# Moving middle blocks as two partition halves in 64 KB runs, from one buffer of three 2-row blocks

## The chip, the cores and the metric

The kernel runs on one core of a Trainium2 chip; the other cores are idle. The metric is the device time of one execution in microseconds (us). The four executions of the kernel before that stand against the changed kernel agree within 0.05%; over all rounds, which ran on several chips, it took 1247.99 to 1252.11 us (0.33%). The granted clock was 1.000. TensorE does next to nothing in this kernel (PE busy for 0.3 us), so that clock plays no part.

## The reference, cut to what matters

```python
def reference(logits, labels):            # (8, 1024, 8192) float32, (8, 1024) int32
    logits_max = np.max(logits, axis=-1, keepdims=True)
    exp_logits = np.exp(logits - logits_max)
    softmax = exp_logits / np.sum(exp_logits, axis=-1, keepdims=True)
    ...                                   # one_hot: 1.0 at labels
    return (softmax - one_hot).astype(np.float32)
```

There are 8192 rows of 8192 floats: 268.4 MB are read and 268.4 MB are written. Each row needs its maximum, its sum of exponentials, a scaling, and a subtraction at one place.

## The kernel before

A tile is 128 rows, one to each partition of SBUF (the memory on the chip that holds the tiles), 32 KB a row, 4 MB a tile. Six tiles fit the buffer. Loads are issued by the sync engine (SP), stores by ScalarE's queue (ACT). VectorE (DVE) does the maximum and the subtraction, ScalarE the exponential and the scaling.

```python
io = ctx.enter_context(tc.tile_pool(name="io", bufs=SLOTS))        # SLOTS = 6
def load(t):
    x = io.tile([P, V], fp32, tag="x", name="x")
    nc.sync.dma_start(out=x[:], in_=x_nv[t * P : (t + 1) * P, :])
    return x
def store(t, x):
    nc.scalar.dma_start(out=o_nv[t * P : (t + 1) * P, :], in_=x[:])
...                                       # row_max, exponent, inverse, normalize, subtract: cut
for t in range(T):                        # T = 64
    s = exponent(xs[t], ms[t])
    r = inverse(s)
    if t + 1 < T:
        xs[t + 1] = load(t + 1)           # waits until the tile six before it has been stored
        ms[t + 1] = row_max(xs[t + 1])
    if t > 0:
        store(t - 1, xs[t - 1])
    normalize(xs[t], r)
    subtract(t, xs[t])
```

## Time and profile before

| | before |
|---|---|
| time, median | 1248.12 us |
| DMA engines, share of the span (two queues) | 50.0% + 49.9% |
| DMA rate, mean | 431 GB/s |
| VectorE busy | 90% |
| one tile in the steady state | 19.35 us |

These are lines of the profile page: busy time, the slices (40 equal parts of the span, busy share in tenths), and the DMA queues (q1 holds the loads, q10 the stores; the last column is the time that their packets took, as a share of 16 engines' span).

```profile
PE 0.3 (0%) x1; PEld 0.2 (0%) x1; DVE 1122.1 (90%) x259; ACT 930.7 (75%) x257; POOL 4.1 (0%) x7
DMA  9999999999999999999999999999999999999998
GB/s 406 421 438 435 424 437 436 435 426 437 435 433 428 437 434 432 429 437 434 432 429 438 435 431 428 438 437 428 431 438 434 429 432 436 435 428 433 437 434 379
DMA packets 18519, 537.00 MB, mean 431 GB/s; under 512 B 2064, under 2 KB 2128, under 8 KB 2128
q1 hardware_dynamic: 9216, 268.44, 50.0%
q10 hardware_dynamic: 9296, 268.51, 49.9%
```

The reader is to see two things: the DMA engines have no idle time, and the rate hardly varies. Next come the waits: who waited for whom, us in total, times, longest. The first line is a compute engine's, the second the sync queue's.

```profile
DVE m L70 <- DMA x<-in_logits_dram: 83.7, 46, 2.4
...
SPq L65 <- DMA out_dram<-x: 1148.9, 58, 66.7
```

VectorE waits for loads only 83.7 us in all. Nearly all of the span, the sync queue waits for a store to land, because a store frees the buffer that the next load needs. A window of the steady state shows busy time by engine, then the granted clock, the DMA share and the rate:

```profile
core 0: us, PE busy (x) PEld busy (x) DVE busy (x) ACT busy (x) POOL busy (x), PEclk, DMA share, GB/s
310.00:620.00 310.00, 0.00 (x0) 0.00 (x0) 281.58 (x65) 235.52 (x66) 0.00 (x0) 1.00 1.00 433
```

In the single transfer records of this trace, a row of 32 KB took 1213 ns on its engine, a run of 1 KB took 46 ns, and a semaphore write 9 ns. A packet is one such run on one of the 16 DMA engines. From 310 to 1150 us 16 packets are in flight at 95% of the instants, and at half of the instants 13 or more of them go the same way, all loads or all stores.

### The profile page before, as it was taken

The page shows a single profiled execution, that of the slowest core. Times are in us where ns is not written, and L with a number is a line of the kernel's source. Part 1 is how long each engine was busy: PE and PEld are TensorE (multiplying, and loading weights), DVE is VectorE, ACT ScalarE, POOL GpSimd, SP SyncE. Part 2 cuts the span into 40 slices and gives each one's busy share as a digit, 9 for nine tenths or more (in the row PEclk, how much of TensorE's full clock was granted, in tenths as well). Part 3 has the DMA queues.
Part 4 walks back from the last instruction along what each step waited for, and adds up shares of the span by engine and source line. Part 5 has one row for each costly group of instructions (what it writes and reads, how often), then busy time and mean ns, then how long its engine had stood idle before and what let it go on. Part 6 is the DMA issues. An engine that isn't in the chain of part 4 may idle for free.

```text
span 1246.1 us, 997 instructions
## 1 busy us (share of the span) xinstructions
PE 0.3 (0%) x1; PEld 0.2 (0%) x1; DVE 1122.1 (90%) x259; ACT 930.7 (75%) x257; POOL 4.1 (0%) x7
## 2 busy tenths in 40 slices
PE   0000000000000000000000000000000000000000
PEld 0000000000000000000000000000000000000000
DVE  3999999999988989889898898988989989889893
ACT  3888888888877777777767777777777777777772
POOL 1000000000000000000000000000000000000000
DMA  9999999999999999999999999999999999999998
GB/s 406 421 438 435 424 437 436 435 426 437 435 433 428 437 434 432 429 437 434 432 429 438 435 431 428 438 437 428 431 438 434 429 432 436 435 428 433 437 434 379
DMA packets 18519, 537.00 MB, mean 431 GB/s; under 512 B 2064, under 2 KB 2128, under 8 KB 2128
## 3 DMA queue, kind: packets, MB, share of 16 engines
q1 hardware_dynamic: 9216, 268.44, 50.0%
q10 hardware_dynamic: 9296, 268.51, 49.9%
q14 instruction: 7, 0.06, 0.0%
HBM read 268.50 MB, written 268.44 MB: 431 GB/s over the span
## 4 chain that ended last, share of the span: by engine, by line
another core or an unknown queue 66%; DVE 21%; DMA 7%; issue 3%; SPq 1%; ACT 1%; DVEq 0%; ACTq 0%
DVE m L70 11%; DVE x L91 10%; DMA out_dram<-x 4%; DMA x<-in_logits_dram 3%; SPq L65 1%; ACT x L75 1%; DVEq L139 0%; ACT x L86 0%; DVE r L80 0%; ACTq L97 0%; DVEq L91 0%; DVEq L70 0%
## 5 line engine op out<-in xcount | busy, mean ns | idle before, releaser
L70 DVE TENSOR_REDUCE m<-x 128x1 f32<-128x8192 f32 x64 | 555.7, 8683 | 83.8 <-DMA x<-in_logits_dram 83.7
L75 ACT ACTIVATE x<-x,m 128x8192 f32<-128x8192 f32 x64 | 455.8, 7122 | 157.0 <-DVE m L70 157.0
L91 DVE SCALAR_TENSOR_TENSOR x<-iota,lab,x 128x4096 f32<-128x4096 int16 x128 | 567.9, 4479 | 4.1 <-ACT x L86 4.1
L86 ACT ACTIVATE x<-x,r 128x4096 f32<-128x4096 f32 x128 | 467.7, 3700 | 123.5 <-DVE r L80 123.5
L80 DVE RECIPROCAL r<-s 128x1 f32<-128x1 f32 x64 | 10.2, 159 | 7.3 <-ACT x L75 7.3
L75 ACT ACTIVATION_READ_ACCUMULATOR x<-x,m 128x1 f32 x64 | 12.0, 187 | 0.0
L75 ACT ACT_TABLE_LOAD x1 | 1.3, 1283 | 13.4 <-DMA x<-in_logits_dram 13.4
L56 DVE CAST lab_f<-lab_raw 64x128 f32<-64x128 int32 x1 | 0.2, 219 | 12.2 <-DMA lab_raw<-in_labels_dram 12.2
L46 POOL IOTA iota<- 128x4096 int16 x1 | 3.5, 3542 | 0.4 <-POOLq L128 0.4
L61 DVE TENSOR_SCALAR lab<-lab_ps 128x64 f32<-128x64 f32 x2 | 0.4, 220 | 0.5 <-PE lab_ps L58 0.5
L58 PE MATMUL lab_ps<-ident,lab_f 64*128 64x64 f32 x1 | 0.3, 338 | 12.5 <-DVE lab_f L56 12.5
L49 POOL TENSOR_SCALAR_AFFINE_SELECT ident<-ident 64x64 f32<-64x64 f32 x1 | 0.2, 234 | 0.1
L58 PEld LDWEIGHTS lab_ps<-ident,lab_f 64*128 64x128 f32 x1 | 0.2, 180 | 12.5 <-issue 12.5
L48 POOL MEMSET ident<- 64x64 f32 x1 | 0.1, 146 | 0.0
L128 POOL MEMSET const-bfloat16-1.0<- 128x1 bf16 x1 | 0.1, 107 | 0.0
L128 POOL MEMSET const-uint8-127<- 128x1 uint8 x1 | 0.1, 107 | 0.0
L128 POOL MEMSET const-float32-0.0<- 128x1 f32 x1 | 0.1, 104 | 0.2 <-issue 0.2
L128 POOL MEMSET const-float32-1.0<- 128x1 f32 x1 | 0.1, 104 | 0.0
## 6 DMA issues: line engine op xcount, KB each, us to landing
x<-in_logits_dram SPq DMA_DIRECT2D x64, 4096.0 KB, 24.2
out_dram<-x ACTq DMA_DIRECT2D x64, 4096.0 KB, 55.0
lab_raw<-in_labels_dram ACTq DMA_DIRECT2D x1, 64.0 KB, 11.4
```

The costliest lines, as they stand in the source:

```text
L46: nc.gpsimd.iota(iota[:], [[1, HALF]], base=0, channel_multiplier=0)
L49: nc.gpsimd.affine_select(out=ident[:], in_=ident[:], compare_op=Alu.not_equal, fill=1.0, base=0, pattern=[[-1, T]], channel_multiplier=1,)
L56: nc.vector.tensor_copy(out=lab_f[:], in_=lab32.rearrange("t (p s) -> t p s", s=step)[:, :, 0])
L58: nc.tensor.transpose(out=lab_ps[:], in_=lab_f[:], identity=ident[:])
L61: nc.vector.tensor_scalar_add(out=lab[:, c, :], in0=lab_ps[:], scalar1=float(-c * HALF))
L65: nc.sync.dma_start(out=x[:], in_=x_nv[t * P : (t + 1) * P, :])
L70: nc.vector.tensor_reduce(out=m[:], in_=x[:], axis=mybir.AxisListType.X, op=Alu.max, negate=True)
L75: nc.scalar.activation(out=x[:], in_=x[:], func=Act.Exp, bias=m[:], scale=1.0, accum_out=s[:])
L80: nc.vector.reciprocal(out=r[:], in_=s[:])
L86: nc.scalar.activation(out=xc, in_=xc, func=Act.Copy, bias=0.0, scale=r[:])
L91: nc.vector.scalar_tensor_tensor(out=xc, in0=iota[:], scalar=lab[:, c, t : t + 1], in1=xc, op0=Alu.is_equal, op1=Alu.subtract, reverse1=True,)
L128: nc = _bacc.Bacc("TRN2", target_bir_lowering=False, num_devices=1)
```

## The change

Partition p of a block now holds two neighbouring rows of the input, so one partition's share of a block is one contiguous run of 64 KB. Middle blocks move as two transfers of 64 partitions (0 to 63, 64 to 127). A half can be loaded again as soon as that half has been stored. Blocks 0 to 4 and 27 to 31 are loaded row by row, blocks 0, 1 and 24 to 31 stored so. Each of the buffer's three places for a block is called a slot. The intent is fewer and longer packets, with freeing fine enough to keep both directions going.

```diff
-SLOTS = 6
+SLOTS = 3
+G = 2
+Q = P // 2
...
+    x_b = x_nv.rearrange("(b p j) v -> b p j v", p=P, j=G)
...
+    X = io.tile([P, SLOTS, G, V], fp32)
+    rows = [(slice(0, P), slice(j, j + 1)) for j in range(G)]
+    halves = [(slice(0, Q), slice(0, G)), (slice(Q, P), slice(0, G))]
+    def parts(b, head, tail):
+        return rows if b < head or b >= B - tail else halves
+    def load(b):
+        for ps, js in parts(b, 5, 5):
+            nc.sync.dma_start(out=X[ps, b % SLOTS, js, :], in_=x_b[b, ps, js, :])
...
+    def store(t):
+        b, j = divmod(t, G)
+        pieces = parts(b, 2, 8)
+        if pieces is rows:
+            pieces = rows[j : j + 1]
+        elif j < G - 1:
+            return
+        for ps, js in pieces:
+            nc.scalar.dma_start(out=o_b[b, ps, js, :], in_=X[ps, b % SLOTS, js, :])
```

The compute instructions keep their shapes and their number; they work on one row of a block at a time. The labels are laid out for the new row order, which costs one small copy and one small matmul more.

More of the change, by code (lines that the diff above doesn't have):

```diff
@@ L31 @@
     T = N // P
+    B = T // G
     C = V // HALF
-    lab_tp = labels.rearrange("a b -> (a b)").rearrange("(t p) -> t p", p=P)
+    lab_bp = labels.rearrange("a b -> (a b)").rearrange("(b q) -> b q", q=G * P)
+    x_b = x_nv.rearrange("(b p j) v -> b p j v", p=P, j=G)
+    o_b = o_nv.rearrange("(b p j) v -> b p j v", p=P, j=G)
     const = ctx.enter_context(tc.tile_pool(name="const", bufs=1))
-    io = ctx.enter_context(tc.tile_pool(name="io", bufs=SLOTS))
+    io = ctx.enter_context(tc.tile_pool(name="io", bufs=1))
     stats = ctx.enter_context(tc.tile_pool(name="stats", bufs=4))
@@ L39 @@
     ctx.enter_context(tc.manual_schedule())
-    lab_raw = const.tile([T, P], labels.dtype)
-    nc.scalar.dma_start(out=lab_raw[:], in_=lab_tp)
+    lab_raw = const.tile([B, G * P], labels.dtype)
+    nc.scalar.dma_start(out=lab_raw[:], in_=lab_bp)
     iota = const.tile([P, HALF], i16)
     nc.gpsimd.iota(iota[:], [[1, HALF]], base=0, channel_multiplier=0)
-    ident = const.tile([T, T], fp32)
+    ident = const.tile([B, B], fp32)
     nc.gpsimd.memset(ident[:], 0.0)
@@ L50 @@
         out=ident[:], in_=ident[:], compare_op=Alu.not_equal, fill=1.0,
-        base=0, pattern=[[-1, T]], channel_multiplier=1,
+        base=0, pattern=[[-1, B]], channel_multiplier=1,
     )
-    lab_f = const.tile([T, P], fp32)
-    lab32 = lab_raw[:].bitcast(i32)
+    lab_f = const.tile([B, G, P], fp32)
     step = mybir.dt.size(labels.dtype) // 4
-    nc.vector.tensor_copy(out=lab_f[:], in_=lab32.rearrange("t (p s) -> t p s", s=step)[:, :, 0])
-    lab_ps = psum.tile([P, T], fp32)
-    nc.tensor.transpose(out=lab_ps[:], in_=lab_f[:], identity=ident[:])
@@ L59 @@
-    lab = const.tile([P, C, T], fp32)
-    for c in range(C):
-        nc.vector.tensor_scalar_add(out=lab[:, c, :], in0=lab_ps[:], scalar1=float(-c * HALF))
-    def load(t):
-        x = io.tile([P, V], fp32, tag="x", name="x")
-        nc.sync.dma_start(out=x[:], in_=x_nv[t * P : (t + 1) * P, :])
-        return x
-    def row_max(x):
+    lab32 = lab_raw[:].bitcast(i32).rearrange("b (p j s) -> b j p s", j=G, s=step)
+    lab = const.tile([P, C, G, B], fp32)
+    lab_ps = psum.tile([P, G, B], fp32)
@@ new lines @@
+    for j in range(G):
+        nc.vector.tensor_copy(out=lab_f[:, j, :], in_=lab32[:, j, :, 0])
+        nc.tensor.transpose(out=lab_ps[:, j, :], in_=lab_f[:, j, :], identity=ident[:])
+    for c in range(C):
+        nc.vector.tensor_scalar_add(out=lab[:, c], in0=lab_ps[:], scalar1=float(-c * HALF))
+    X = io.tile([P, SLOTS, G, V], fp32)
[3 more added lines that the diff above has]
+        return rows if b < head or b >= B - tail else halves
@@ L69, in row_max, with row, exponent @@
+    def load(b):
+        for ps, js in parts(b, 5, 5):
+            nc.sync.dma_start(out=X[ps, b % SLOTS, js, :], in_=x_b[b, ps, js, :])
+    def row(t):
+        return X[:, t // G % SLOTS, t % G, :]
+    def row_max(t):
         m = stats.tile([P, 1], fp32, tag="m", name="m")
-        nc.vector.tensor_reduce(out=m[:], in_=x[:], axis=mybir.AxisListType.X, op=Alu.max, negate=True)
+        nc.vector.tensor_reduce(out=m[:], in_=row(t), axis=mybir.AxisListType.X, op=Alu.max, negate=True)
         return m
-    def exponent(x, m):
+    def exponent(t, m):
@@ L74, in exponent @@
         s = stats.tile([P, 1], fp32, tag="s", name="s")
-        nc.scalar.activation(out=x[:], in_=x[:], func=Act.Exp, bias=m[:], scale=1.0, accum_out=s[:])
+        nc.scalar.activation(out=row(t), in_=row(t), func=Act.Exp, bias=m[:], scale=1.0, accum_out=s[:])
         return s
@@ L81, in inverse, with normalize, subtract @@
         return r
-    def normalize(x, r):
+    def normalize(t, r):
         for c in range(C):
-            xc = x[:, c * HALF : (c + 1) * HALF]
+            xc = row(t)[:, c * HALF : (c + 1) * HALF]
             nc.scalar.activation(out=xc, in_=xc, func=Act.Copy, bias=0.0, scale=r[:])
-    def subtract(t, x):
+    def subtract(t):
         for c in range(C):
-            xc = x[:, c * HALF : (c + 1) * HALF]
+            xc = row(t)[:, c * HALF : (c + 1) * HALF]
             nc.vector.scalar_tensor_tensor(
-                out=xc, in0=iota[:], scalar=lab[:, c, t : t + 1], in1=xc,
+                out=xc, in0=iota[:], scalar=lab[:, c, t % G, t // G : t // G + 1], in1=xc,
                 op0=Alu.is_equal, op1=Alu.subtract, reverse1=True,
             )
-    def store(t, x):
-        nc.scalar.dma_start(out=o_nv[t * P : (t + 1) * P, :], in_=x[:])
-    xs, ms = {}, {}
-    xs[0] = load(0)
-    ms[0] = row_max(xs[0])
+    def store(t):
[7 more added lines that the diff above has]
+            nc.scalar.dma_start(out=o_b[b, ps, js, :], in_=X[ps, b % SLOTS, js, :])
+    load(0)
+    m = row_max(0)
     for t in range(T):
-        s = exponent(xs[t], ms[t])
+        s = exponent(t, m)
         r = inverse(s)
         if t + 1 < T:
-            xs[t + 1] = load(t + 1)
-            ms[t + 1] = row_max(xs[t + 1])
+            if (t + 1) % G == 0:
+                load((t + 1) // G)
+            m = row_max(t + 1)
         if t > 0:
-            store(t - 1, xs[t - 1])
-        normalize(xs[t], r)
-        subtract(t, xs[t])
-    store(T - 1, xs[T - 1])
+            store(t - 1)
+        normalize(t, r)
+        subtract(t)
+    store(T - 1)
 _INS = ['logits', 'labels']
```

## The prediction

The forecast came to 1246 us, from a best case of about 1243, with about 3 us saved on packets, and up to 20 us that coarser freeing might add. (b): the risk that a half, as such, moves more slowly. (b) had no term in the 1246; it stands in the odds (about one in five) and in the signs to look for.

> **What bounds it now: the 16 DMA engines.** The page: DMA share in tenths is 9 in 39 of 40 slices; the two queues take 50.0% and 49.9% of the 16 engines' span; 537 MB at a mean of 431 GB/s. From about 310 us the windows show 433 GB/s, DMA share 1.00, VectorE 90% busy. In the timeline a tile then takes 19.35 us (8.39 MB, 433 GB/s); earlier, while six buffers fill, it takes 17.45 us, which is VectorE (8.58 for the max, 8.87 for the subtract). The sync queue's waits put 1149 us on stores landing; a store takes 55.0 us from issue to landing, a load 24.2. So compute has slack (VectorE waits only 83.7 us for loads in all) and the transfers have none.
>
> **What can be saved.** Single DMA records: a 32 KB row takes 1213 ns, a 1 KB row 46 ns, a semaphore write 9 ns. That fits about 8 ns per packet plus 27.2 GB/s per engine, 435 GB/s for 16[...]. The kernel runs at 99.5% of it. Blocks 5 to 26 load and 2 to 23 store as 64 KB runs: 5632 packets fewer, times 8 ns, over 16 engines, is about 3 us. Start (12.6 us for the first load) and end (last store 1229.97 to 1246) stay row by row, so unchanged. Engine work is unchanged: 64 x 17.45 = 1117 us. Best case about 1243 us[...].
>
> **What it adds.** (a) Freeing gets coarser. Row 0 of a block waits for row 1 before it is stored. The cycle of a slot, by estimate: store both halves 38.7 us (at half the DMA rate), load the second half 19.35, landing to store issue 52.4 (three VectorE tile-times), some 4 to 5 us of latencies: about 115.5, against 3 x 38.7 = 116.1 available. It just fits, with next to no slack where before there were tens of us; a miss costs perhaps 1 us per block, up to 20 us in all.
> (b) [...] In the trace now, 13 to 16 engines are on loads at the same instant, then on stores[...]. No run here shows that limit. I give it about one in five: the uneven row-wise ends (2 store blocks first, 5 load blocks last) look like values found on the chip, which a collapse of the middle would not have let stand.
>
> **Prediction.** 1246 us, 8 in 10 between 1239 and 1290. Faster by over 2%: 0.05; within 2%: 0.68; slower by over 2%: 0.27.
>
> **What would show it.** Right: about 12,900 DMA packets instead of 18,519; 64 KB packets near 2418 ns; middle slices still 430 to 436 GB/s with DMA share 1.00; VectorE's waits for loads moved to every second tile, so the same sum or slightly more. (a) wrong: gaps of several us before the row max at each block's first row, DMA share under 0.98. (b) wrong: 64 KB packets of 3 to 5 us with a DMA share still 1.00 and GB/s far below 430.
>
> **What would make it wrong.** [...] latencies of store landing and load issue longer than I assumed; or another engine rate in 64 KB packets or with one half loading while the other stores (faster).

## The result

| | before | after |
|---|---|---|
| time, median | 1248.12 us | 1699.25 us (1697.32 to 1717.23, 4 runs) |
| ratio | | 1.3646, 95% interval 1.3553 to 1.3738 |
| DMA rate, mean | 431 GB/s | 317 GB/s |
| DMA packets | 18519 | 12854 |
| VectorE's waits for loads | 83.7 us | 501.4 us |

A ratio here is the mean time of one kernel's runs over that of the other's of the same rounds, so it is not quite the ratio of the medians quoted. Executions over 1.5% slower than the fastest of the same kernel are left out of the means.

The same lines of the page after the change, and its DMA issues (last column: us from issue to landing):

```profile
PE 0.4 (0%) x2; PEld 0.3 (0%) x2; DVE 1122.8 (66%) x260; ACT 929.0 (55%) x257; POOL 4.0 (0%) x7
DMA  9999999999999999999999999999999999999998
GB/s 410 421 433 306 314 281 275 303 289 295 300 278 274 277 292 292 284 281 283 277 274 294 275 286 292 257 303 272 318 269 283 286 291 278 408 431 433 433 432 387
DMA packets 12854, 536.99 MB, mean 317 GB/s; under 512 B 2064, under 2 KB 2064, under 8 KB 2096
q1 hardware_dynamic: 6400, 268.44, 57.6%
q10 hardware_dynamic: 6448, 268.51, 41.6%
...
out_dram<-X ACTq DMA_DIRECT2D x44, 47.2
X<-in_logits_dram SPq DMA_DIRECT2D x44, 37.1
```

The line to look at is GB/s. It is above 400 in the first three slices and in the last six but the final one (387, the run-out), where blocks move row by row, and about 285 in between, where they move as halves. Yet the DMA line says 9 in all slices but the last: the engines are not waiting, they are slow. Two windows of the middle and two waits say the same:

```profile
200.00:1350.00 1150.00, 0.00 (x0) 0.00 (x0) 677.73 (x154) 552.30 (x153) 0.00 (x0) 1.00 0.99 285
700.00:900.00 200.00, 0.00 (x0) 0.00 (x0) 126.84 (x30) 101.95 (x29) 0.00 (x0) 1.00 1.00 278
...
DVE m L91 <- DMA X<-in_logits_dram: 501.4, 28, 37.9
...
SPq L84 <- DMA out_dram<-X: 1580.9, 58, 58.1
```

From 200 to 1350 us the window reads 285 GB/s at a DMA share of 0.99. Those 328 MB would have taken 757 us at 433 GB/s; they took 1150. That is 393 of the 451 us lost; most of the rest falls in the transitions on both sides. VectorE's busy time is unchanged (1122.8 us against 1122.1). It waits, for 15 to 38 us at the first row of a middle block.

The single records show where the time sits:

```
mean ns of one packet       loads    stores    (all of that size in the run)
before,  32 KB               1216      1213
after,   64 KB               4420      2896    (fastest 2418 in both)
```

A 64 KB packet can take 2418 ns, twice 1213 less 8. The typical load packet took nearly twice that. Summed over the 16 engines from 200 to 1350 us, the time of the 64 KB packets beyond 2418 ns comes to 385 us (314 of loads, 71 of stores), and the idle time to 8 us. So the 393 us lost there are long packets, and hardly any waiting.

### The profile page after: what moved, and what is told of

Same layout as the page of the kernel before. It is cut to its first block, busy times and chain, and to the rows that moved or that the text cites. A ratio compares the mean times of both kernels' runs of the same rounds, so it can differ in the third digit from the quotient of the medians.

```text
span 1695.5 us, 877 instructions
## 1 busy us (share of the span) xinstructions
PE 0.4 (0%) x2; PEld 0.3 (0%) x2; DVE 1122.8 (66%) x260; ACT 929.0 (55%) x257; POOL 4.0 (0%) x7
## 2 busy tenths in 40 slices
DMA packets 12854, 536.99 MB, mean 317 GB/s; under 512 B 2064, under 2 KB 2064, under 8 KB 2096
## 4 chain that ended last, share of the span: by engine, by line
DMA 52%; DVE 25%; another core or an unknown queue 19%; issue 1%; ACT 1%; SPq 0%; DVEq 0%; ACTq 0%
DMA out_dram<-X 26%; DMA X<-in_logits_dram 25%; DVE m L91 13%; DVE X L112 12%; ACT X L96 0%; SPq L84 0%; DVEq L168 0%; ACT X L107 0%; DVE r L101 0%; DVEq L91 0%; ACTq L125 0%; DVEq L112 0%
## 5 line engine op out<-in xcount | busy, mean ns | idle before, releaser
L91 DVE TENSOR_REDUCE m<-X 128x1 f32<-128x8192 f32 x64 | 555.2, 8675 | 501.4 <-DMA X<-in_logits_dram 501.4
L96 ACT ACTIVATE X<-X,m 128x8192 f32<-128x8192 f32 x64 | 455.6, 7118 | 554.7 <-DVE m L91 554.4
L112 DVE SCALAR_TENSOR_TENSOR X<-iota,lab,X 128x4096 f32<-128x4096 int16 x128 | 567.9, 4478 | 18.5 <-ACT X L107 18.4
L107 ACT ACTIVATE X<-X,r 128x4096 f32<-128x4096 f32 x128 | 467.6, 3700 | 180.6 <-issue 127.8
L96 ACT ACTIVATION_READ_ACCUMULATOR X<-X,m 128x1 f32 x64 | 12.0, 187 | 0.0
```

The source lines that it names most:

```text
L91: nc.vector.tensor_reduce(out=m[:], in_=row(t), axis=mybir.AxisListType.X, op=Alu.max, negate=True)
L96: nc.scalar.activation(out=row(t), in_=row(t), func=Act.Exp, bias=m[:], scale=1.0, accum_out=s[:])
L107: nc.scalar.activation(out=xc, in_=xc, func=Act.Copy, bias=0.0, scale=r[:])
L112: nc.vector.scalar_tensor_tensor(out=xc, in0=iota[:], scalar=lab[:, c, t % G, t // G : t // G + 1], in1=xc, op0=Alu.is_equal, op1=Alu.subt ...
```

## The experiments

The theory to test: the rate of a transfer depends on **which partitions** it covers, and 0 to 63 and 64 to 127 are slow sets. Forecasts that stand without a rival's name are those of this theory. Three rivals: (1) runs of 64 KB are slow in themselves; (2) any transfer of fewer than 128 partitions is slow; (3) the coarser freeing of the buffer makes the loss.

### Transfers alone, one direction

This kernel has no arithmetic and a wrong result. Phases follow each other in one execution, so they can be compared with one another. Each of the four kernels of transfers alone ran once.

```diff
+    loads(ROW, range(0, 6));  loads(WHOLE, range(6, 12))        # 128 x 32 KB; 128 x 64 KB
+    loads(LOW, range(12, 18)); loads(BOTH, range(18, 24))       # partitions 0-63; both halves in turn
+    loads(MID, range(24, 30))                                   # partitions 32-95
+    stores(...)                                                 # the same five, in the same order
```

> A kernel of transfers alone (its result is wrong on purpose): six blocks (50.3 MB; 25.2 MB where one half alone moves) loaded five ways one after the other, then stored the same five ways: rows of 128 partitions x 32 KB; whole blocks of 128 x 64 KB; the lower half (partitions 0 to 63) alone, 64 x 64 KB; both halves in turn; and partitions 32 to 95, 64 x 64 KB. [...] loads of rows and whole blocks near 430 GB/s,[...] and of partitions 32 to 95[...] near 430 again. Whether stores obey the same limit is open: packets in the changed kernel averaged 4420 ns for loads but 2896 for stores, so I expect stores of halves[...] perhaps near 400. Rival 1 (64 KB runs are slow): whole blocks and partitions 32 to 95 are slow too. Rival 2 (any transfer of 64 partitions is slow): whole blocks fast, partitions 32 to 95 as slow as the lower half. Rival 3 (the slowness is coarse freeing and waits): all ways near 430.

Windows inside the phases (the columns are us, POOL, clock, DMA share, GB/s). In order: loads of rows, whole blocks, the lower half, both halves in turn, partitions 32 to 95; then stores of the same five (the last window is short, 20 us).

```profile
20.00:100.00 80.00, 0.00 (x0) 1.00 1.01 433
130.00:230.00 100.00, 0.00 (x0) 1.00 0.99 430
260.00:350.00 90.00, 0.00 (x0) 1.00 1.02 210
440.00:590.00 150.00, 0.00 (x0) 1.00 0.98 203
615.00:640.00 25.00, 0.00 (x0) 1.00 0.98 422
680.00:760.00 80.00, 0.00 (x0) 1.00 1.01 435
800.00:880.00 80.00, 0.00 (x0) 1.00 1.01 436
910.00:1000.00 90.00, 0.00 (x0) 1.00 1.02 210
1080.00:1200.00 120.00, 0.00 (x0) 1.00 0.99 238
1260.00:1280.00 20.00, 0.00 (x0) 1.00 1.02 442
```

Halves run at about half the rate in both directions: loads at 210 and 203 GB/s against 433 of the rows, stores at 210 against 435 (both halves in turn a little faster, 238), with 64 KB packets of the lower half of about 5115 ns for loads and 5100 ns for stores. Whole blocks with the same 64 KB runs are at full rate (430 and 436), which rules out rival 1. Partitions 32 to 95 are also 64 partitions in 64 KB runs, and run at full rate, both ways (422 and 442). This rules out rival 2. What sets that slice apart is which partitions it holds. My guess that stores alone would be less hurt was wrong: 210 GB/s.

### Transfers alone, both directions

> Transfers alone again (wrong result on purpose), loads and stores at once from different buffers, eight phases: rows and rows; whole and whole; lower half loads with lower half stores; lower half loads with upper half stores; both halves in turn for both; partitions 32 to 95 for both; row loads with half stores; half loads with row stores. [...] phases 1, 2 and 6 at 430 to 435 GB/s in total; phases 3, 4 and 5 at about 280, as the changed kernel's middle; phase 8 (half loads) slow, 64 KB load packets over 4000 ns, phase 7 (half stores) closer to full speed. [...] Rival 1 (64 KB runs): phases 2 and 6 slow. Rival 2 (64 partitions): 6 slow, 2 fast. Rival 3 (waits): all full.

```diff
+    phase(1, ROW, ROW, 4);   phase(0, WHOLE, WHOLE, 4)
+    phase(1, LOW, LOW, 6);   phase(0, LOW, HIGH, 6)     # loads, stores
+    phase(1, BOTH, BOTH, 4); phase(0, MID, MID, 6)
+    phase(1, ROW, BOTH, 4);  phase(0, BOTH, ROW, 4)
```

The eight phases in that order:

```profile
90.00:190.00 100.00, 0.00 (x0) 1.00 1.00 433
220.00:370.00 150.00, 0.00 (x0) 1.00 1.00 433
385.00:530.00 145.00, 0.00 (x0) 1.00 0.99 291
560.00:700.00 140.00, 0.00 (x0) 1.00 1.00 299
735.00:900.00 165.00, 0.00 (x0) 1.00 0.99 323
945.00:1020.00 75.00, 0.00 (x0) 1.00 1.00 433
1060.00:1210.00 150.00, 0.00 (x0) 1.00 0.99 334
1280.00:1400.00 120.00, 0.00 (x0) 1.00 0.99 288
```

Only phases with a half of 0 to 63 or 64 to 127 in them are slow (288 to 334 GB/s; the others read 433). Loading and storing the same half (291) is about as fast as loading one half and storing the other (299), so the intended picture, one half going out while the other comes in, buys nothing. With both directions the rate is above 210 but far below 433. Phases 7 and 8 show that one direction in halves is enough to take much of the rate (334 with half stores, 288 with half loads, against 433); I had expected phase 7, half stores, to be closer to full speed, and it was not (334).

### The buffer and the freeing without the halves

```diff
-        for ps, js in parts(b, 5, 5):
+        for ps, js in parts(b, B, 0):
-        pieces = parts(b, 2, 8)
+        pieces = parts(b, B, 0)
```

> The changed kernel with every block moved row by row: the new buffer, the new row order and the freeing by row stay, the halves and the 64 KB runs go. [...] both transfer rivals: 1246 to 1252 us, DMA 430 GB/s. Rival 3 (the buffer of three blocks and its freeing cost the time): clearly above 1300.

It took 1248.63 us, ratio 1.0003 (0.9988 to 1.0018) to the kernel before, and correct. Window of its steady state:

```profile
300.00:1150.00 850.00, 0.00 (x0) 0.00 (x0) 772.09 (x177) 639.03 (x177) 0.00 (x0) 1.00 1.00 433
```

So the new buffer, the new row order and freeing by row cost nothing. Everything lost is in the middle blocks' pieces.

### 64 KB runs without the halves

```diff
-    halves = [(slice(0, Q), slice(0, G)), (slice(Q, P), slice(0, G))]
+    halves = [(slice(0, P), slice(0, G))]
```

> The changed kernel with the middle blocks moved whole, 128 partitions x 64 KB in one transfer of 8 MB, so 64 KB runs without halves. [...] 64 KB packets at 2418 ns when a transfer moves; the time is set by the coarser freeing alone (a slot cycle of some 135 us against 116, less because a lone transfer runs at full rate), 1255 to 1390 us, so faster than the changed kernel. Rival 1 (64 KB runs slow): packets over 3000 ns and 1700 us or more. Rival 3 (coarse freeing is the cause): slower than the changed kernel, as the freeing is coarser still, with full-speed packets.

It took 1330.67 us, ratio 1.0659 (1.0642 to 1.0677): freeing is coarser than in the changed kernel, and it is still 369 us faster. This contradicts rival 3.

```profile
300.00:900.00 600.00, 0.00 (x0) 0.00 (x0) 494.26 (x113) 411.05 (x114) 0.00 (x0) 1.00 0.96 395
```

Here the DMA share falls to 0.96, which is what waiting looks like, and what the changed kernel's 0.99 did not show. Waiting is only half of it: in these 600 us the engines were idle for 26, and load packets beyond 2418 ns took 27 more. Store packets averaged 2418 ns, load packets 2644; the slow ones came in bursts near the start of a load or its end, for a reason that I did not look into. So some packets are slow without halves too, but by far less (27 us in 600, against 385 in 1150).

### One direction in halves at a time

Half loads with stores row by row (only `parts(b, 2, 8)` becomes `parts(b, B, 0)`):

> The changed kernel with half loads kept and all stores row by row. [...] from the mixed transfers (half loads with row stores 288 GB/s): 369 MB of the middle take 1281 us plus 390, about 1670 us, so nearly all of the loss. If loads and stores of halves each cost about a half: about 1470.

Half stores with loads row by row (only `parts(b, 5, 5)` becomes `parts(b, B, 0)`):

> The changed kernel with half stores kept and all loads row by row. [...] from the mixed transfers (row loads with half stores 334 GB/s): 369 MB take 1105 us plus 390, about 1495 us. If only loads were hurt[...]: about 1250.

Half loads took 1662.67 us, ratio 1.3315 (1.3160 to 1.3470), close to what the transfers alone had promised. Half stores took 1602.25, ratio 1.2831 (1.2794 to 1.2869), 107 us more than I expected. Each direction by itself loses most of the 451 us (414 and 354), so the parts do not add up: with one direction in halves the engines are already held up. The long packets are those of the direction in halves: 4597 ns on average for the half loads and 4144 for the half stores, while the 32 KB packets of the other direction averaged 1268 and 1275.

### Halves with 32 KB runs

```diff
+    halves = [(slice(h, h + Q), slice(j, j + 1)) for h in (0, Q) for j in range(G)]
```

> The changed kernel's halves with 32 KB runs: the middle blocks move as four pieces of 64 partitions x one row (2 MB). [...] the run length does not matter, so 32 KB load packets of the middle average over 2000 ns instead of 1213 and the middle runs at 280 to 300 GB/s; 1640 to 1720 us. Rival 1 (64 KB runs are the cause, already contradicted by the transfers alone): about 1250 us.

It took 1517.09 us, ratio 1.2149 (1.2093 to 1.2206). The expectation failed: halves are slow with 32 KB runs too, but 182 us less slow than with 64 KB runs. One kernel was made to see why.

> Transfers alone again (wrong result on purpose), to settle why 64 partitions x 32 KB (the changed kernel with 32 KB runs, 331 GB/s in its middle) lost less than 64 x 64 KB (285). The lower half alone, one direction at a time, in 32 KB and in 64 KB runs; then both directions: lower half in 64 KB runs, in 32 KB runs, both halves in 64 KB runs, in 32 KB runs, and row loads of 128 partitions with lower-half stores in 32 KB runs. [...] one direction alone gives 205 to 215 GB/s with either run[...]. With both directions, if the shorter packet by itself[...], 32 KB runs give 320 to 340 GB/s against 290 to 325 for 64 KB; if the order of the four pieces in the kernel did it, equal rates.

```diff
+    loads(LOW32, range(6)); stores(LOW32, range(6))             # 64 x 32 KB, one direction
+    loads(LOW, range(6), (1, 0, 2)); stores(LOW, range(6), (2, 0, 1))
+    phase(0, LOW, LOW, 6);   phase(1, LOW32, LOW32, 6)
+    phase(0, BOTH, BOTH, 4); phase(1, BOTH32, BOTH32, 4)
+    phase(0, ROW, LOW32, 6)
```

One direction alone gave 208 to 210 GB/s with either run. Both directions, in the order lower half 64 KB, lower half 32 KB, both halves 64 KB, both halves 32 KB:

```profile
545.00:650.00 105.00, 0.00 (x0) 1.00 1.00 310
705.00:820.00 115.00, 0.00 (x0) 1.00 1.00 326
870.00:960.00 90.00, 0.00 (x0) 1.00 1.01 312
1090.00:1230.00 140.00, 0.00 (x0) 1.00 1.00 369
```

So shorter packets alone recover a part where the halves alternate (369 against 312). With one half the gain (326 against 310) is not clear: the same phase in 64 KB runs read 291 in the kernel of both directions above. The last phase, row loads with lower-half stores in 32 KB runs, read 393 (1255 to 1370 us). Why shorter packets recover it is not shown.

### Another cut of the partitions

```diff
+    halves = [(slice(32, 96), slice(0, G)), (slice(0, 32), slice(0, G)), (slice(96, P), slice(0, G))]
```

> The changed kernel with other pieces: partitions 32 to 95[...] in one transfer, 0 to 31 and 96 to 127[...] in two, all in 64 KB runs. [...] half of the middle's bytes at 433 GB/s and half at about 295, the rates of the mixed transfers: 426 + 625 us for 369 MB, plus some 390 us for the ends, so 1440 to 1560 us, clearly faster than the changed kernel though a block now takes three transfers. Rival 2 (transfers of fewer than 128 partitions are slow): as slow as the changed kernel or slower.

The one fast run took 1542.72 us; the other, the profiled one, took 1578.15 and counts as slow, so there is no interval. The fast run is 157 us below the changed kernel with three transfers to a block in place of two, and inside the expected range.

### Other slices of the partitions

> Transfers alone, one direction (wrong result on purpose): [...] other slices, all in 64 KB runs. [...] partitions 64 to 127[...]: 203 to 212 GB/s, packets near 5115 ns as the lower half; 0 to 31[...]: the same rate though the slice is half as large; 0 to 15[...]: about 105 GB/s, packets near 10,000 ns; 16 to 79[...]: half of the packets near 5115 ns and half near 2418, the total held to about 210 GB/s by the slow ones; 32 to 95[...]: 430 GB/s. Rival (the number of partitions sets the rate): 0 to 31 half of the lower half's rate, 16 to 79 and 32 to 95 equal, packets all alike within a slice.

```diff
+    loads(span(0, 128), range(0, 3));  loads(span(64, 128), range(3, 9))
+    loads(span(0, 32), range(9, 15));  loads(span(0, 16), range(15, 21))
+    loads(span(16, 80), range(21, 27)); loads(span(32, 96), range(0, 6))
+    stores(span(0, 16), range(0, 6)); stores(span(0, 32), range(6, 12)); stores(span(16, 80), range(12, 18))
```

Loads of partitions 64 to 127, 0 to 31, 0 to 15 and 16 to 79:

```profile
70.00:170.00 100.00, 0.00 (x0) 1.00 1.02 209
195.00:235.00 40.00, 0.00 (x0) 1.00 1.03 210
245.00:285.00 40.00, 0.00 (x0) 1.00 0.97 105
364.00:405.00 41.00, 0.00 (x0) 1.00 1.00 208
```

Partitions 0 to 31 run as fast as 64 to 127 (210 and 209 GB/s), and 0 to 15 at half that (105, packets of 9635 ns): the number of partitions does not set the rate. For 16 to 79 I had expected about 210 GB/s in total, half of the packets near 5115 ns and half near 2418. The stores came in two such groups: between 555 and 600 us, with no load in flight, 127 of 202 packets took under 2500 ns and 70 took 5000 to 5150. The loads did not: between 364 and 405 us, with no store in flight, all 130 took 4900 to 5150 ns, and the rate was 208. Why loads and stores of this slice differ is not shown. Later stores and loads ran at once in this kernel, so its load phase of 32 to 95 can't be read.

### Versions that keep all 128 partitions and coarsen one direction

Whole middle stores, loads row by row:

> A version that should beat both: the changed kernel with all loads row by row and the middle stores whole, 128 partitions x 64 KB, 2816 packets fewer at 8 ns over 16 engines, 1.4 us. [...] no packet is slowed; what is left is the slot cycle, 38.7 store + 19.35 load + 52.4 + some 5, 115.5 against 116.1: 1246 to 1265 us. Coarse freeing of one direction costing as much as of both: 1290 or more.

Whole middle loads, stores row by row:

> The mirror: all stores row by row, the middle loads whole, 128 partitions x 64 KB. The second row's store 19.35 + load 38.7 + 52.4 + some 5: 115.5 against 116.1: 1246 to 1265 us. Coarse freeing of one direction costing as much as of both: 1290 or more.

```diff
-    halves = [(slice(0, Q), slice(0, G)), (slice(Q, P), slice(0, G))]
+    halves = [(slice(0, P), slice(0, G))]
-        pieces = parts(b, 2, 8)            # e8; e7 changes the loads' line instead
+        pieces = parts(b, B, 0)
```

Whole stores took 1316.65 us, ratio 1.0520 (1.0489 to 1.0551), outside the 1246 to 1265 that I had expected: my sum for the slot's cycle gave the same 115.5 us for both. That store of 8 MB is issued after the second row only and the next loads wait for all of it. But waiting is the smaller part: in the 900 us of the first window below the engines were idle for 13, and packets longer than 1213 and 2418 ns added 28 (about half of it in each direction), though I had written that no packet is slowed. Why this version loses 68 us and the mirror nothing was not tested. Whole loads took 1248.06 us, ratio 1.0000 (0.9986 to 1.0013), with 433 GB/s in its middle (second window):

```profile
300.00:1200.00 900.00, 0.00 (x0) 0.00 (x0) 764.12 (x176) 636.09 (x176) 0.00 (x0) 1.00 0.99 413
300.00:1150.00 850.00, 0.00 (x0) 0.00 (x0) 779.17 (x180) 646.65 (x179) 0.00 (x0) 1.00 1.00 433
```

So 64 KB load packets at 128 partitions do no harm, and the 1.4 us that they might save is below what these runs resolve. No version that I ran beats the kernel before.

## Why the prediction was wrong

**What bounds the kernel: right.** The DMA engines do; after the change, too, they are never idle for long (share 0.99), but held up. The estimate of about 8 ns a packet held: a 64 KB packet took 2418 ns at its fastest, and on average for the stores of whole blocks, as worked out, and the packet count fell to 12,854 (12,900 predicted). The saving of 3 us was never to be had at the halves' rate.

**(a) Coarser freeing up to 20 us: not the cause.** The sign I named, gaps before the row max at each block's first row, did appear (VectorE waited 501.4 us, in 28 waits). But the DMA share stayed at 0.99, so the gaps come from slow transfers, not from idle ones: 385 us of long packets against 8 us of idle time in the middle. Where freeing was really coarse and no halves were moved (whole blocks), the loss was 82 us in all, in the middle about half of it idle time (share 0.96) and half longer load packets. Freeing by row cost nothing (1248.63 us).

**(b) Slow halves: the step that failed.** The forecast charged 2418 ns for every 64 KB packet, in halves too, and so kept the middle at 430 to 436 GB/s. In the middle load packets took 4420 ns and store packets 2896, and the rate was 285. The risk was named, and its odds were wrong. As its sign the prediction gave 64 KB packets of 3 to 5 us with a DMA share still 1.00 and GB/s far below 430; loads averaged 4.4 us and stores 2.9, at 0.99 and 285. But it gave this "about one in five", because the uneven ends "look like values found on the chip". That was reasoning about an author, and no run had moved a half by then. What the prediction says beside it of the trace of before, 13 to 16 engines on loads and then on stores, was too strong: 13 or more packets go the same way at half of the instants, more than 8 at 98% of them. By itself that says nothing of halves. The runs showed 209 to 210 GB/s for one direction of one half, against 433 for rows. 1246 us, and the range up to 1290, rested on the wrong branch.

**Both directions at once** did not save the halves. With both in halves, in 64 KB runs, transfers alone reached 291 to 323 GB/s, above the 209 to 210 of one half in one direction and far below the 433 of rows; why they lie between is not shown.

**What stays open.** In the changed kernel load packets suffer more (4420 ns) than store packets (2896), while each direction alone suffers alike (5115 and 5100). Its 285 GB/s is also below the 312 and 323 of both halves in turn without arithmetic. Open, too, is why all load packets of 16 to 79 were slow (4900 to 5150 ns) and only 70 of 202 store packets (5000 to 5150). That the partitions moved decide the rate is shown, for the slices that were moved; by what mechanism is not.

## What to carry to other kernels

A transfer of fewer than 128 partitions is judged by which partitions it covers, and that is measured: moved alone, 0 to 63 and 64 to 127 halved the rate here (loads at 210 and 209 GB/s against 433 of rows), 32 to 95 did not (422). Split a block along its rows, keeping all 128 partitions, when it must be freed in parts; that cost nothing here (1248.63 us against 1248.22 of the kernel before in the same round). A DMA share near 1.00 is no sign of health by itself (0.99 at 285 GB/s here): read it together with GB/s and with the time of one packet, and when a risk that could make the kernel much slower has not been measured, don't overrule it with a guess that somebody must have measured it; one run of transfers alone showed it here.
